# Two column tiles for the DeltaNet inverse's larger levels and for the samples' state products

## The chip, the cores and the metric

One Trainium2 chip, one NeuronCore of it. The metric is the device time of one execution in microseconds; of several runs the median is given.

## The reference

The reference is one layer of a streaming encoder for 256 prompt positions and 64 sample positions, 320 in all, with width 2048, in float32. It normalises, multiplies by one large input matrix, runs a convolution module beside a gated DeltaNet of 8 heads (head size 128), multiplies by an output matrix, and ends with a convolutional feed-forward block. The change lies in the DeltaNet, where for each chunk of positions a unit lower triangular matrix is inverted, and each sample head is started from a given state:

```python
m = jnp.where(strict, jnp.einsum('bhnid,bhnjd->bhnij', kb, k) * decay, 0.0)
tmat = lax.linalg.triangular_solve(m + eye, ..., left_side=True, lower=True, unit_diagonal=True)
...
def step(s, xs):
    v_new = u_c - jnp.einsum('bhld,bhde->bhle', w_c, s)
    o = jnp.einsum('bhld,bhde->bhle', qd_c, s) + jnp.einsum('bhij,bhje->bhie', qk_c, v_new)
    s = s * gl_c[..., None, None] + jnp.einsum('bhld,bhle->bhde', kd_c, v_new)
    return s, o
```

The kernel takes prompt chunks of 128 positions, and one sample chunk of 64 per head.

## The kernel before

The large products (input, output, up and down projection) run as dense streams on TensorE: a block of weights is 128x128 and stationary, the activations of all 320 positions stream past it. Each product is done three times on split numbers (high by high, low by high, high by low; lines 233, 234 and 237 of `block_matmul`). The weights come by DMA into `w`, ScalarE rounds them to `whi` (L217) and VectorE computes the rest `wlo` (L218); three buffers of each are kept.

The DeltaNet runs in between, in small steps. `tick` counts the dense matmuls, and after every 20 of them lets the jobs that are due issue their next step behind the last dense matmul; a `yield LAG_WAIT, ...` in a job says how many dense matmuls have to pass before its next step. So TensorE's order is fixed when the program is built: some dense matmuls, a group of small ones, dense ones again. The order on ScalarE and VectorE comes from the scheduler's own estimate and from priorities; each engine works its queue in order.

Heads go in pairs, four pairs in all. For one pair, `st` holds five instances (NI = 5): two prompt chunks of each of two heads (S_ = 4), and one instance in which the samples of the two heads stand one below the other, 64 rows each. `base_inverse` inverts the 16-row diagonal blocks on VectorE. `levels` then joins blocks to 32, 64 and 128 rows. In one level, for the two halves r0 (above) and r1 (below) of a block: `pz` = a product on the rows of r0, copied to `zq`; `px` and `py` = products of `zq` on the rows of r1, copied into `W` (the inverse, transposed) and `TT` (the inverse). `N` is the matrix `m`, tile `np`; `W` and `TT` are the two halves of tile `wtp`. The level that joins 16-row blocks is L792 to L808; the level of 32 rows is L815 (pz), L817 (copies to zq), L822 (px), L824 (py), L825 and L827 (copies); the level of 64 rows is L831, L832, L836, L837. All those products are float32.

Below, the partitions that a small matmul reads are called its row strip, those that it writes its column strip, and the two together its tile. In the code before, every instance of a level uses the same one or two tiles.

`post` uses the inverse. `vn0` is the first chunk's new values (`pvn`, L864). `ks` (L881) holds the samples' key and query products with the two states `s0`: both heads' samples (128 rows of `kqs`) are multiplied with both heads' states (256 columns), and of the result only the half is read in which a head's samples meet its own state. VectorE makes `rhs_` of it (L885) and ScalarE `qss` (L886), one instruction for each head. `rhs_` goes into `pvns` (L893).

Of the kernel before, what the change touches and what calls it, by code (L numbers as in the profile page):

```python
# [11 lines left out]
AF = mybir.ActivationFunctionType  # L12
ALU = mybir.AluOpType
# [4 lines left out]
P = 128  # L18
# [3 lines left out]
TS = 64  # L22
# [54 lines left out]
S_ = 4  # L77
# [23 lines left out]
def trunk_kernel(ctx, tc, ins, outs):  # L101
    nc = tc.nc
    V, S, G, PE = nc.vector, nc.scalar, nc.gpsimd, nc.tensor
# [94 lines left out]
    def cv(name, n=P, m=P):  # L198
        o, _ = CST[name]
        return cst[0:n, o:o + m] if o < NCST1 else cst2[0:n, o - NCST1:o - NCST1 + m]  # L200
# [115 lines left out]
    with tc.tile_pool(name="xp", bufs=1) as xp:  # L316
# [71 lines left out]
        for k0 in range(0, KB, 2):  # L388
            hi, lo = pre[k0 // 2]
            for ks in ((k0,), (k0 + 1,)) if k0 < 4 else ((k0, k0 + 1),):  # L390
                for wt in (hi, lo):
                    for k in ks:
                        for i, b in enumerate(FIRST):
                            ps = ready[b][:, 0:T]
                            o = (k - k0) * FW + i * P
# [214 lines left out]
    NI = S_ + 1  # L610
# [166 lines left out]
    zq = gd.tile([P, NI, TS], F32, tag="zq", bufs=1, name="zq")  # L777

    def levels(st):
        N, W, TT = st["np"], st["w"][:, 0, :, :], st["w"][:, 1, :, :]  # L780

        def out(name, n, w):
            return ps_g.tile([P, 512], F32, tag="g", name=name)[:, 0:n * w].rearrange("p (a w) -> p a w", a=n)


        q = [slice(32 * i, 32 * i + 32) for i in range(4)]
        even = [slice(32 * i, 32 * i + 16) for i in range(4)]
        odd = [slice(32 * i + 16, 32 * i + 32) for i in range(4)]
        pz = out("pz", NI, 16)
        for a in range(NI):  # L790
            for r, c in zip(q, even):
                PE.matmul(pz[r, a, :], N[r, a, r], TT[r, a, c], start=True, stop=True)  # L792
        S.activation(zh, pz, AF.Identity, scale=cv("odd", P, 1))
        yield LAG_WAIT, 2, 0
        px, py = out("px", NI, 16), out("py", NI, 16)
        for a in range(NI):
            for r, e, c in zip(q, even, odd):
                PE.matmul(px[e, a, :], zh[r, a, :], W[r, a, c], start=True, stop=True)
        for a in range(NI):
            for i, r in enumerate(q[:3]):  # L800
                if i != 1 or a < S_:
                    PE.matmul(py[r, a, :], W[r, a, r], zh[r, a, :], start=True, stop=True)
        for i, (r, e) in enumerate(zip(q, even)):
            if i < 3:
                n = S_ if i == 1 else NI
                V.tensor_tensor(TT[r, 0:n, e], TT[r, 0:n, e], py[r, 0:n, :], ALU.add)
        for i, (e, c) in enumerate(zip(even, odd)):
            S.copy(W[e, :, c], px[e, :, :])  # L808
        yield LAG_ADD, 1, 0

        pairs32 = (q[0:2], q[2:4])
        pz = out("pz", NI, 32)
        for a in range(NI):
            for r0, r1 in pairs32:
                PE.matmul(pz[r1, a, :], N[r0, a, r1], TT[r0, a, r0], start=True, stop=True)  # L815
        for r0, r1 in pairs32:
            S.copy(zq[r1, :, 0:32], pz[r1, :, :])  # L817
        yield LAG_WAIT, 2, 0
        px, py = out("px", NI, 32), out("py", S_, 32)
        for a in range(NI):  # L820
            for r0, r1 in pairs32:
                PE.matmul(px[r0, a, :], zq[r1, a, 0:32], W[r1, a, r1], start=True, stop=True)  # L822
        for a in range(S_):
            PE.matmul(py[q[1], a, :], W[q[1], a, q[1]], zq[q[1], a, 0:32], start=True, stop=True)  # L824
        S.copy(TT[q[1], 0:S_, q[0]], py[q[1], :, :])  # L825
        for r0, r1 in pairs32:
            S.copy(W[r0, :, r1], px[r0, :, :])  # L827
        yield LAG_ADD, 1, 0
        pz = out("pz", S_, 64)
        for a in range(S_):  # L830
            PE.matmul(pz[64:P, a, :], N[0:64, a, 64:P], TT[0:64, a, 0:64], start=True, stop=True)  # L831
        S.copy(zq[64:P, 0:S_, :], pz[64:P, :, :])  # L832
        yield LAG_WAIT, 1, 0
        px = out("px", S_, 64)
        for a in range(S_):
            PE.matmul(px[0:64, a, :], zq[64:P, a, :], W[64:P, a, 64:P], start=True, stop=True)  # L836
        S.copy(W[0:64, 0:S_, 64:P], px[0:64, :, :])  # L837

    def post(i, st):
        hh_ = (2 * i, 2 * i + 1)  # L840
        kq, kqs, kd, vh, at, W = st["kq"], st["kqs"], st["kd"], st["vh"], st["at"], st["w"][:, 0, :, :]
        kds = kdss[i % 2]
        rk, rq, irk, snb, cc, skd = (st["sc"][:, j, :] for j in range(6))
        eG, neG, eGl = gate["eG"], gate["neG"], gate["eGl"]

        def pair_tile(tag, n=2):
            return gd.tile([P, n, P], F32, tag=tag, bufs=1, name=tag)

        def bank(name, n):
            return ps_g.tile([P, 512], F32, tag="g", name=name)[:, 0:n * P].rearrange("p (a f) -> p a f", a=n)  # L850

        s0 = pair_tile("s0")
# [16 lines left out]
        def outputs(c, vn):  # L869
            p = bank("po", 4)  # L870
            for s in range(2):
                PE.matmul(p[:, 2 + s, :], kd[:, 2 * s + c, :], vn[:, s, :], start=True, stop=True)
            for s in range(2):
                PE.matmul(p[:, s, :], at[:, 2 * s + c, :], vn[:, s, :], start=True, stop=True)
            return p

        vn0 = new_values(0, [vh[:, 2 * s, :] for s in range(2)])

        p = bank("ks", 4)
        for j in range(2):  # L880
            PE.matmul(p[:, 2 * j:2 * j + 2, :], kqs[:, j, :], s0, start=True, stop=True)  # L881
        rhs_, qss = pair_tile("rhs", 1)[:, 0, :], pair_tile("qss", 1)[:, 0, :]
        for s in range(2):
            r = slice(s * TS, (s + 1) * TS)
            V.scalar_tensor_tensor(rhs_[r, :], p[r, s, :], neG[r, 2, hh_[1]:hh_[1] + 1], vh[r, S_, :], ALU.mult, ALU.add)  # L885
            S.activation(qss[r, :], p[r, 2 + s, :], AF.Identity, scale=eG[r, 2, hh_[1]:hh_[1] + 1])  # L886
        yield LAG_WAIT, 2, 0
        p = outputs(0, vn0)
        sn0 = pair_tile("sn0")
# [2 lines left out]
        p = bank("pvns", 1)  # L892
# [6 lines left out]
        p = bank("ks1", 4)  # L899
# [8 lines left out]
        p = bank("pos", 3)  # L908
# [11 lines left out]
        p = outputs(1, vn1)  # L920
# [21 lines left out]
        for s in range(2):  # L942

            pt = ps_t.tile([P, 512], F32, tag="t", name="pt_o")
            o = TP - s * TS
# [15 lines left out]
    def pair(i, st):  # L961
        while any(s not in st for s in range(NS)):
            yield GAP, 0, 0
        yield from base_inverse(i, st)
        yield LAG_BASE - 5 * GAP, 1, 0
        yield from levels(st)
        while i and any(j is pairs[i - 1] for j in jobs):
            yield GAP, 2, 0
        yield LAG_WAIT, 2, 0
        yield from post(i, st)  # L970
# [75 lines left out]
    for n in range(KB):  # L1046
# [11 lines left out]
        for j in range(nk2):  # L1058
            xh, xl = bx(K1 + j)
            o = j * P  # L1060
# [164 lines left out]
    for step in PLAN_Y.split():  # L1225
        how, ks = step[0], step[1:]
# [97 lines left out]
```

## Time and profile before

| | |
|---|---|
| median of three runs | 1489.62 us (1489.47 to 1491.08) |
| the profiled execution's own time | 1489.37 us |
| its span, first to last instruction | 1487.6 us |
| TensorE busy, share of the span | 1478.6 us, 99% |
| VectorE busy | 996.6 us, 67% |
| ScalarE busy | 730.8 us, 49% |
| the four visits to the levels and to `post` | between 160 and 427 us |
| in 160 to 420 us: VectorE busy, ScalarE busy | 225.7 and 146.6 of 260 us |

Busy times of TensorE overlap, since its matmuls are pipelined: a group of small matmuls is read by its starts, not by its busy time. In the profile's rows PE is TensorE, PEld its weight loads, DVE is VectorE, ACT is ScalarE, SP the engine that issues DMAs; L815 is line 815 of the kernel before. A row of the timeline merges consecutive instructions of one line; its second column reaches from the first start to the last end. A bracket at the end of a row gives the idle time ahead of the first of them and who ended it.

### The profile page before, as it was taken

The numbers are of one execution on the slowest core, as the hardware profiler recorded it, in microseconds if no ns is written. First come the engines' busy times: TensorE is split into PE (matmuls) and PEld (weight loads), VectorE is DVE, ScalarE is ACT, GpSimd is POOL, SyncE is SP. The second block draws the span as 40 slices with busy tenths as digits, with TensorE's granted clock in tenths as the row PEclk, the third lists the DMA queues.
The fourth block names the chain that finished last, engine by engine and source line by source line (L and its number), as shares of the span: only waits on it lengthen the run. The fifth ranks groups of instructions, "written<-read, shape, count | busy, mean of one in ns | idle before, by whom it ended". The sixth has DMA issues, their size and how long they took to land.

```text
span 1487.6 us, 27264 instructions
## 1 busy us (share of the span) xinstructions
PE 1478.6 (99%) x10610; PEld 1458.2 (98%) x10610; DVE 996.6 (67%) x1816; ACT 730.8 (49%) x1331; POOL 230.5 (15%) x390
## 2 busy tenths in 40 slices
PE   9999999999999999999999999999999999999998
PEld 8999999999999989999999999999999999999997
DVE  6779888888989678756336665545666545656554
ACT  7674556655454656544334444334444334444453
POOL 0111101021010000322002322002232001223101
PEclk9999999999999999999999999999999999999999
DMA  8435453544444734444554444554444455444453
GB/s 294 140 115 167 158 151 110 147 156 138 129 122 145 238 128 146 146 156 121 153 168 155 145 154 135 143 162 158 156 143 147 136 148 168 153 156 143 136 148 119
DMA packets 98281, 224.22 MB, mean 151 GB/s; under 512 B 18792, under 2 KB 39528, under 8 KB 98152
## 3 DMA queue, kind: packets, MB, share of 16 engines
q1 hardware_dynamic: 98008, 222.45, 47.8%
q8 instruction: 83, 1.36, 0.4%
q14 instruction: 46, 0.38, 0.1%
q10 hardware_dynamic: 144, 0.03, 0.0%
HBM read 215.33 MB, written 7.12 MB: 150 GB/s over the span
## 4 chain that ended last, share of the span: by engine, by line
PE 95%; ACT 2%; DVE 1%; issue 1%; DMA 0%; POOL 0%; DVEq 0%; ACTq 0%; POOLq 0%
PE psu L237 13%; PE psu L234 13%; PE psu L233 13%; PE psdn L233 7%; PE psdn L234 7%; PE psdn L237 7%; PE psq L233 3%; PE psq L234 3%; PE psq L237 3%; PE psm L237 2%; PE psm L233 2%; PE psm L234 2%; PE psu L1117 1%; PE psv L233 1%; PE psgate L233 1%; PE ps_first L398 1%
## 5 line engine op out<-in xcount | busy, mean ns | idle before, releaser
L217 ACT CAST whi<-w 128x1024 fp32r<-128x1024 f32 (+2 forms) x440 | 412.6, 940 | 488.5 <-PE psu L234 169.7
L218 DVE TENSOR_TENSOR wlo<-w,whi 128x1024 fp32r<-128x1024 f32 (+2 forms) x440 | 477.2, 1085 | 191.4 <-ACT whi L217 123.9
L233 PE MATMUL psu<-hi,whi 128*128 128x320 f32 x1344 | 397.0, 309 | 0.0
L234 PE MATMUL psu<-lo,whi 128*128 128x320 f32 x1344 | 396.9, 309 | 0.0
L234 PEld LDWEIGHTS psu<-lo,whi 128*128 128x128 f32 x1344 | 252.3, 188 | 0.0
L233 PEld LDWEIGHTS psu<-hi,whi 128*128 128x128 f32 x1344 | 252.2, 188 | 0.0
L237 PE MATMUL psu<-hi,wlo 128*128 128x320 f32 x1344 | 224.4, 309 | 0.0
L237 PEld LDWEIGHTS psu<-hi,wlo 128*128 128x128 f32 x1344 | 204.1, 188 | 0.0
L234 PE MATMUL psdn<-gl,whi 128*128 128x320 f32 x660 | 195.9, 310 | 0.0
L1150 POOL COPY nffn<-fbuf 128x2 f32<-128x2 f32 x88 | 99.5, 1131 | 586.7 <-DVE fbuf L1148 583.5
L1148 DVE TENSOR_TENSOR fbuf<-psu,rb 128x256 f32<-128x256 f32 x88 | 37.4, 424 | 169.1 <-PE psu L237 169.0
L233 PE MATMUL psdn<-gh,whi 128*128 128x320 f32 x480 | 142.8, 309 | 0.0
L234 PEld LDWEIGHTS psdn<-gl,whi 128*128 128x128 f32 x660 | 123.9, 188 | 0.3
L233 PE MATMUL psq<-hh,whi 128*128 128x320 f32 x352 | 106.0, 314 | 0.0
L234 PE MATMUL psq<-hl,whi 128*128 128x320 f32 x352 | 104.1, 309 | 0.0
L233 PEld LDWEIGHTS psdn<-gh,whi 128*128 128x128 f32 x480 | 90.1, 188 | 0.0
L237 PE MATMUL psdn<-gh,wlo 128*128 128x320 f32 x480 | 89.9, 309 | 0.0
L237 PEld LDWEIGHTS psdn<-gh,wlo 128*128 128x128 f32 x480 | 75.3, 188 | 0.0
L233 PEld LDWEIGHTS psq<-hh,whi 128*128 128x128 f32 x352 | 66.1, 188 | 0.4
L234 PEld LDWEIGHTS psq<-hl,whi 128*128 128x128 f32 x352 | 66.1, 188 | 0.2
L563 DVE SCALAR_TENSOR_TENSOR cvt<-ub,par,cvt 128x320 f32<-128x320 f32 x120 | 65.3, 545 | 0.1
L1193 DVE TENSOR_TENSOR y<-y,psdn 128x320 f32<-128x320 f32 x45 | 22.0, 488 | 58.7 <-PE psdn L237 58.7
(356 smaller groups left out, 2485.2 us busy)
## 6 DMA issues: line engine op xcount, KB each, us to landing
w<-in_w_up SPq DMA_DIRECT2D x176, 512.0 KB
w<-in_w_in SPq DMA_DIRECT2D x88, 512.0 KB
w<-in_w_down SPq DMA_DIRECT2D x64, 384.0 KB
w<-in_w_down SPq DMA_DIRECT2D x64, 320.0 KB
w<-in_w_out SPq DMA_DIRECT2D x32, 320.0 KB
w<-in_w_out SPq DMA_DIRECT2D x16, 384.0 KB
w<-in_w_first SPq DMA_DIRECT2D x6, 512.0 KB
wtp<-wsp SPq DMA_DIRECT2D x4, 640.0 KB
```

What stands on the lines that cost most here:

```text
L217: S.copy(hi[:, 0:width], w[:, 0:width])
L218: V.tensor_tensor(lo[:, 0:width], w[:, 0:width], hi[:, 0:width].bitcast(F32), ALU.subtract)
L233: tick(PE.matmul(ps, wh, xh, start=(first and k0 + j == 0), stop=False))
L234: tick(PE.matmul(ps, wh, xl, start=False, stop=False))
L237: tick(PE.matmul(ps, lo[:, j * P:(j + 1) * P], xh, start=False, stop=(final and k0 + j == nk - 1)))
L398: tick(PE.matmul(ps, w, xh, start=(k == 0 and wt is hi), stop=(k == KB - 1 and wt is lo)))
L563: return lambda: V.scalar_tensor_tensor(acc, x, w, acc, ALU.mult, ALU.add)
L1117: PE.matmul(pss[i][:, 0:T], wt[:, o:o + P], x, start=(k == 0 and n == 0), stop=(k == KB - 1 and n == 2))
L1148: V.tensor_tensor(buf[:, 2:258], psu[:, 0:TP], rb2[:, 0:TP], ALU.mult)
L1150: G.tensor_copy(nffn[:, b, 0, :], buf[:, 256:258])
L1193: V.tensor_tensor(y[:, n, :], y[:, n, :], psd[:, 0:T], ALU.add)
```

## The change

In the levels of 32 and 64 rows, instance `a` writes its product to one column strip if `a` is even and to another if it is odd. In the 32-row level `pz` goes to the strip of r1 or r0, `px` to that of r0 or r1, `py` to the third or fourth strip. In the 64-row level the two halves alternate. So half of the products land in PSUM on other partitions than those on which they are needed, and ScalarE's copies, one for the even and one for the odd instances, bring them there: a copy reads 32 or 64 partitions and writes others. Six copies per visit become twelve, each of half the instances or so.

The samples' state products are done for each head alone: 64 rows of `kqs` with that head's 128 state columns, written to the 64 partitions of that head's samples. So `ks` has two columns of 128 where it had four, and `rhs_` and `qss` are one instruction of 128 partitions each.

```diff
         for a in range(NI):
-            for r0, r1 in pairs32:
-                PE.matmul(pz[r1, a, :], N[r0, a, r1], TT[r0, a, r0], start=True, stop=True)
-        for r0, r1 in pairs32:
-            S.copy(zq[r1, :, 0:32], pz[r1, :, :])
+            for rs in pairs32:
+                PE.matmul(pz[rs[1 - a % 2], a, :], N[rs[0], a, rs[1]], TT[rs[0], a, rs[0]], start=True, stop=True)
+        for rs in pairs32:
+            for o in range(2):
+                S.copy(zq[rs[1], o:NI:2, 0:32], pz[rs[1 - o], o:NI:2, :])
         yield LAG_WAIT, 2, 0
         px, py = out("px", NI, 32), out("py", S_, 32)
         for a in range(NI):
-            for r0, r1 in pairs32:
-                PE.matmul(px[r0, a, :], zq[r1, a, 0:32], W[r1, a, r1], start=True, stop=True)
+            for rs in pairs32:
+                PE.matmul(px[rs[a % 2], a, :], zq[rs[1], a, 0:32], W[rs[1], a, rs[1]], start=True, stop=True)
         for a in range(S_):
-            PE.matmul(py[q[1], a, :], W[q[1], a, q[1]], zq[q[1], a, 0:32], start=True, stop=True)
-        S.copy(TT[q[1], 0:S_, q[0]], py[q[1], :, :])
-        for r0, r1 in pairs32:
-            S.copy(W[r0, :, r1], px[r0, :, :])
+            PE.matmul(py[q[2 + a % 2], a, :], W[q[1], a, q[1]], zq[q[1], a, 0:32], start=True, stop=True)
+        for o in range(2):
+            S.copy(TT[q[1], o:S_:2, q[0]], py[q[2 + o], o:S_:2, :])
+        for rs in pairs32:
+            for o in range(2):
+                S.copy(W[rs[0], o:NI:2, rs[1]], px[rs[o], o:NI:2, :])
         yield LAG_ADD, 1, 0
+        half = (slice(0, 64), slice(64, P))
         pz = out("pz", S_, 64)
         for a in range(S_):
-            PE.matmul(pz[64:P, a, :], N[0:64, a, 64:P], TT[0:64, a, 0:64], start=True, stop=True)
-        S.copy(zq[64:P, 0:S_, :], pz[64:P, :, :])
+            PE.matmul(pz[half[1 - a % 2], a, :], N[0:64, a, 64:P], TT[0:64, a, 0:64], start=True, stop=True)
+        for o in range(2):
+            S.copy(zq[64:P, o:S_:2, :], pz[half[1 - o], o:S_:2, :])
...
-            PE.matmul(px[0:64, a, :], zq[64:P, a, :], W[64:P, a, 64:P], start=True, stop=True)
-        S.copy(W[0:64, 0:S_, 64:P], px[0:64, :, :])
+            PE.matmul(px[half[a % 2], a, :], zq[64:P, a, :], W[64:P, a, 64:P], start=True, stop=True)
+        for o in range(2):
+            S.copy(W[0:64, o:S_:2, 64:P], px[half[o], o:S_:2, :])
...
-        p = bank("ks", 4)
+        p = bank("ks", 2)
         for j in range(2):
-            PE.matmul(p[:, 2 * j:2 * j + 2, :], kqs[:, j, :], s0, start=True, stop=True)
+            for s in range(2):
+                r = slice(s * TS, (s + 1) * TS)
+                PE.matmul(p[r, j, :], kqs[:, j, r], s0[:, s, :], start=True, stop=True)
...
-        for s in range(2):
-            r = slice(s * TS, (s + 1) * TS)
-            V.scalar_tensor_tensor(rhs_[r, :], p[r, s, :], neG[r, 2, hh_[1]:hh_[1] + 1], vh[r, S_, :], ALU.mult, ALU.add)
-            S.activation(qss[r, :], p[r, 2 + s, :], AF.Identity, scale=eG[r, 2, hh_[1]:hh_[1] + 1])
+        V.scalar_tensor_tensor(rhs_, p[:, 0, :], neG[:, 2, hh_[1]:hh_[1] + 1], vh[:, S_, :], ALU.mult, ALU.add)
+        S.activation(qss, p[:, 1, :], AF.Identity, scale=eG[:, 2, hh_[1]:hh_[1] + 1])
```

What stands in the engines' queues now. ScalarE at the fourth visit, from the copies of the first 32-row product on; `zT` is the gate of a head, `un` and `sg` belong to the convolution module, `CAST whi` are the weights. Before:

```order
L217 CAST whi<-w 128x1024 x2
L817 COPY zq<-pz 32x5x32 x2
L959 ACTIVATE zT_5113<-zT_5113 128x320
L217 CAST whi<-w 128x1024
L827 COPY wtp<-px 32x5x32
L825 COPY wtp<-py 32x4x32
L827 COPY wtp<-px 32x5x32
L591 ACTIVATE un<-pt_c,gnm,grs 128x128 x3
```

And now:

```order
L217 CAST whi<-w 128x1024 x2
L818 COPY zq<-pz 32x3x32
L818 COPY zq<-pz 32x2x32
L818 COPY zq<-pz 32x3x32
L965 ACTIVATE zT_5136<-zT_5136 128x320
L818 COPY zq<-pz 32x2x32
L217 CAST whi<-w 128x1024
L830 COPY wtp<-px 32x3x32
L827 COPY wtp<-py 32x2x32 x2
L830 COPY wtp<-px 32x2x32
L830 COPY wtp<-px 32x3x32
L830 COPY wtp<-px 32x2x32
```

The two copies to `zq` are four, and the fourth stands behind the activation `zT`. In the other three visits the four stand together.

VectorE at the third visit, around the samples' `rhs`; `cvt` and `odd` are the convolution's taps, `tmp` and `wi` the base inverse of the next pair. Before:

```order
L218 TENSOR_TENSOR wlo<-w,whi 128x1024
L563 SCALAR_TENSOR_TENSOR odd<-ub_587,par,odd 128x320
L563 SCALAR_TENSOR_TENSOR cvt<-ub_587,par,cvt 128x320
L885 SCALAR_TENSOR_TENSOR rhs<-ks,neG,vh 64x128
L563 SCALAR_TENSOR_TENSOR odd<-ub_587,par,odd 128x320
L885 SCALAR_TENSOR_TENSOR rhs<-ks,neG,vh 64x128
L754 TENSOR_TENSOR tmp<-wi,dn 40x50
```

And now:

```order
L218 TENSOR_TENSOR wlo<-w,whi 128x1024
L563 SCALAR_TENSOR_TENSOR odd<-ub_587,par,odd 128x320
L891 SCALAR_TENSOR_TENSOR rhs<-ks,neG,vh 128x128
L754 TENSOR_TENSOR tmp<-wi,dn 40x50
L563 SCALAR_TENSOR_TENSOR cvt<-ub_587,par,cvt 128x320
```

One instruction takes the place of two and stands one tap earlier; the taps behind it move by a place. On TensorE no group changes its place: the order is that of before, with four `ks` matmuls of 64x128 where two of 128x256 stood. GpSimd's queue and the DMA queue have the same instructions in the same order.

## The prediction

> **What bounds the kernel now.** I read the page first: which engine is busy, and on whose work the chain that ended last lies.
>
> ```profile
> span 1487.6 us, 27264 instructions
> PE 1478.6 (99%) x10610; PEld 1458.2 (98%) x10610; DVE 996.6 (67%) x1816; ACT 730.8 (49%) x1331; POOL 230.5 (15%) x390
> ...
> PE 95%; ACT 2%; DVE 1%; issue 1%; DMA 0%; POOL 0%; DVEq 0%; ACTq 0%; POOLq 0%
> ```
>
> TensorE carries 95% of the chain. So a nanosecond that the change takes out of TensorE's stream is worth a nanosecond, as long as nobody else is then late. I take the next rows from the timeline of TensorE at the first of four visits (one per pair of heads) to the inverse's levels. Columns: start, time from the first start to the last end, engine, line, tiles, shape, count.
>
> ```profile
> 172.06 0.50 PE L815 MATMUL pz<-wtp,np 32*32 32x32 f32 x20
> ...
> 175.62 0.41 PE L822 MATMUL px<-wtp,zq 32*32 32x32 f32 x14
> 175.84 0.21 PE L824 MATMUL py<-zq,wtp 32*32 32x32 f32 x1
> 175.86 0.22 PE L822 MATMUL px<-wtp,zq 32*32 32x32 f32 x3
> 175.90 0.19 PE L824 MATMUL py<-zq,wtp 32*32 32x32 f32 x1
> 175.90 0.22 PE L822 MATMUL px<-wtp,zq 32*32 32x32 f32 x2
> 175.93 0.19 PE L824 MATMUL py<-zq,wtp 32*32 32x32 f32 x1
> 175.93 0.19 PE L822 MATMUL px<-wtp,zq 32*32 32x32 f32 x1
> 175.96 0.32 PE L824 MATMUL py<-zq,wtp 32*32 32x32 f32 x5
> ```
>
> The program has 10 matmuls on L815, and the trace 20 records: each float32 matmul is two passes. The last five passes of L824 run alone on one tile, one every (0.32 - 0.19) / 4 = 0.032 us, since one pass shows 0.19. L815 uses two row strips, hence two tiles of ten passes each; its starts spread over 0.50 - 0.19 = 0.31 us, that is ten passes at 0.032. So a tile takes one pass per 0.032 us, and tiles run beside each other.
>
> The rows from 175.84 on carry the whole forecast. L824 reads partitions 32 to 63 and writes partitions 32 to 63. Half of L822's matmuls read the same partitions 32 to 63 and write 0 to 31. L824's first three passes (175.84, 175.90, 175.93) fall among the last six of L822, and L822 does not slow down. Two column tiles on the same rows therefore did run at once.
>
> How often this is paid, by the rows of two lines (count, then min/median/max ns, then first and last start):
>
> ```profile
> L836 PE MATMUL px<-wtp,zq x32: 218/218/267, 186.3 to 407.1; 64*64 64x64 f32 x32
> L881 PE MATMUL ks<-s,kqs x16: 379/379/382, 190.4 to 411.7; 128*128 128x256 f32 x16
> ```
>
> 32 and 16 records are four visits of 8 and 4, from 186 to 412 us. The 32-row lines come in the same four visits.
>
> **The change part by part, TensorE.** The 32-row product (L815): instances 0, 2, 4 stay on their column tile, 1 and 3 go to a free one. The longest tile has 3 x 2 = 6 passes in place of 10, so 4 x 0.032 = 0.126 us go per visit.
>
> The 32-row second products (L822, L824): before, the starts run from 175.62 to 175.96 + 0.32 - 0.19 = 176.09, 0.47 us. After, L822 takes 6 passes, and L824 has two tiles of 4. L824's passes began when 14 of L822's 20 had begun; with four tiles that comes after about four passes a tile, at 0.13 us. Four passes more end the group at 0.27 to 0.28 us: 0.19 us saved. This has row strip 32 to 63 feeding up to four column strips; the trace shows two. If only two go at once, L824's eight passes last 0.25 us and the saving is 0.09 us.
>
> The 64-row products (L831, L836), from the timeline at 186 us:
>
> ```profile
> 186.29 0.68 PE L836 MATMUL px<-wtp,zq 64*64 64x64 f32 x8
> 186.89 0.41 PE L233 MATMUL psq<-hh,whi 128*128 128x320 f32 x1
> 187.15 0.30 PE L234 MATMUL psq<-hl,whi 128*128 128x320 f32 x1
> ```
>
> Eight passes stand on one tile; their starts spread over 0.68 - 0.22 = 0.46 us, 0.058 a pass after the first. With two tiles four passes go, less a few ns between the tiles: 0.227 us for each of the two lines, 0.454 a visit.
>
> The samples' state products (L881), which come behind L864 (rows of the first visit):
>
> ```profile
> 189.93 0.60 PE L864 MATMUL pvn<-vh,wtp 128*128 128x128 f32 x4
> 190.37 1.03 PE L881 MATMUL ks<-s,kqs 128*128 128x256 f32 x4
> 191.05 0.50 PE L233 MATMUL psq<-hh,whi 128*128 128x320 f32 x1
> 191.38 0.31 PE L234 MATMUL psq<-hl,whi 128*128 128x320 f32 x1
> ```
>
> Here the matmuls leave full-array form, and that has a price. Going from full-array to narrow tiles is shown elsewhere:
>
> ```profile
> 242.27 0.49 PE L578 MATMUL pt_c<-cst,cvt 128*128 128x128 f32 x3
> 242.69 0.68 PE L836 MATMUL px<-wtp,zq 64*64 64x64 f32 x8
> ```
>
> Full-array passes of 128 columns follow each other every (190.37 - 189.93) / 4 = 0.11 us. L578's third therefore starts at 242.49, and L836 comes 0.20 us behind it in place of 0.11: 0.09 us for the switch. Coming back costs 0.14 us from L836's last start (186.75) to the dense matmul and 0.26 to the next, 0.40; a stream of 128 columns in place of 64 adds 0.053, so 0.45 after the new ks. Today L881's last start is 191.40 - 0.38 = 191.02, and the second dense matmul comes 0.36 us later. Passes: four of 0.216 (1.03 - 0.38 over three steps) become four on each of two tiles of 0.11, the step of L864; the first pass of a narrow group shows 0.05 more. Before, from L864's last start: 0.11 + 3 x 0.216 + 0.36 = 1.12 us. After: 0.20 + 0.05 + 3 x 0.11 + 0.01 + 0.45 = 1.04. So 0.08 us go. No row shows column tiles with all 128 rows. If they overlap and the first pass hides, 0.13 go; if they don't, eight passes in a row make it 0.35 us dearer. I take 0.08, since L822 beside L824 is the nearest row.
>
> Sum per visit: 0.126 + 0.191 + 0.454 + 0.083 = 0.854 us, times four is 3.42 us.
>
> The rule that speaks against this is in the Trainium skill, page "TensorE: Matmul & The Clock Gate", Part 3, "What overlaps and what doesn't": a weight load overlaps a running matmul only if its row group is another one. By it the new column tiles, which share their rows, would gain nothing; the rows at 175.84 to 175.93 disagree. It is the third case below.
>
> **ScalarE and VectorE.** The copies out of PSUM are split in two. Their durations:
>
> ```profile
> L817 ACT COPY zq<-pz x8: 283/285/287, 172.6 to 393.3; 32x160 f32<-32x160 f32 x8
> L825 ACT COPY wtp<-py x4: 257/257/259, 176.5 to 397.3; 32x128 f32<-32x128 f32 x4
> L837 ACT COPY wtp<-px x4: 367/367/367, 187.6 to 407.4; 64x256 f32<-64x256 f32 x4
> ```
>
> 32 elements less make 28 ns less. So 96 and 64 elements take about 229 and 201 ns: each pair of zq or px copies grows from 570 to 860, py's from 257 to 402, each 64-row copy from 367 to 2 x 255. That is 0.29 + 0.29 + 0.15 + 0.29 = 1.0 us per visit on ScalarE, against which one activation of qss falls away. Half of the new copies go to other partitions than they read. No row has that; it can't be cheaper than the same elements in place, and I bound it at 0.47, the 128x320 activation below. Either hides: zq is copied by 393.6 at the last visit and read at 396.3 (rows below), 2.7 us later, and even four copies at 0.47 fit.
>
> VectorE does one rhs of 128 rows in place of two of 64:
>
> ```profile
> L885 DVE SCALAR_TENSOR_TENSOR rhs<-ks,neG,vh 64x128 f32<-64x128 f32 x8 | 2.8, 349 | 2.1 <-PE ks L881 1.5 <-ACT qss L886 0.4
> ```
>
> That is 0.35 us less per visit, and a wait between the two engines goes. None of it is on the chain.
>
> Behind the four visits the chain leaves TensorE once for long, at the output projection:
>
> ```profile
> 499.72 0.16 PE psm L1063
> 499.92 0.73 ACT whi L217
> ...
> 506.61 6.44 DMA w<-in_w_out
> ```
>
> That transfer is issued behind casts which begin 0.04 us after a matmul (499.92). So it moves forward with TensorE, and the gain passes through it.
>
> What is late next? At the last visit the fourth zq copy is now queued behind zT on ScalarE (front part, first order listing), and zT waits for VectorE. The rows of before, ScalarE, then TensorE, then VectorE:
>
> ```profile
> 393.00 0.59 ACT L817 COPY zq<-pz 32x160 f32<-32x160 f32 x2 [0.54 <-PE pz L815]
> 395.51 0.47 ACT L959 ACTIVATE zT<-zT 128x320 f32<-128x320 f32 x1 [1.92 <-DVE zT L958]
> ```
> ```profile
> 396.30 0.38 PE L822 MATMUL px<-wtp,zq 32*32 32x32 f32 x12
> ```
> ```profile
> 342.11 0.49 DVE L536 TENSOR_TENSOR sg<-psgate,rb 128x320 f32<-128x320 f32 x1 [0.35 <-PE psgate L237]
> 369.69 1.23 DVE L218 TENSOR_TENSOR wlo<-w,whi 128x1024 fp32r<-128x1024 f32 x1 [2.64 <-ACT whi L217]
> 394.99 0.49 DVE L958 TENSOR_TENSOR zT<-psz,rb 128x320 f32<-128x320 f32 x1
> ```
>
> In the times of before, the fourth copy would end at 395.98 + 0.20 = 396.18, 0.12 us ahead of L822. TensorE will come there 3 x 0.854 + 0.126 = 2.69 us earlier. So the copy must move as far, and it hangs on VectorE, which from 370 to 408 us is nearly without a gap:
>
> ```profile
> 370.00:408.00 38.00, 37.60 (x75) 1.00 0.41 123
> ```
>
> VectorE itself waited for TensorE at 342.11. By then 1.71 us of two visits and 0.77 of the third are saved, 2.48; with the shorter rhs behind it, 2.5 to 2.9. The copy is then 0 to 0.1 us late. I take 0.1 off: 3.3 us.
>
> **The rivals.**
>
> A, the forecast: 3.3 us less. The profiled execution took 1489.37 us, 1.8 of it outside the span; 3.3 off is 1486.1. The median of before, 1489.62, is 0.25 above that execution, so 1486.3. Own range: L824 at 0.09 saved and ks at nothing leave 2.6 us (1487.0); ks at 0.13 and no stall give 3.6 (1486.0); the runs of before spread over 1.6 us, which I let widen it to 1485.2 to 1487.6.
>
> B, given back at the last visit: VectorE does not follow, and zT holds the fourth copy and with it L822. If VectorE has gained only its own 0.35 by then, L822 stands for 2.69 - 0.12 - 0.35 = 2.2 us and 1.2 us of the gain are left: 1488.4. For it: 37.60 busy of 38 us. Against: the waits at 342.11 and 369.69, where VectorE could start earlier. It decides from about 2.6 us of lead on. The Trainium skill has this as a general warning ("TensorEngine Tiling (Array Packing)", "PSUM Bottleneck"): tiling speeds up TensorE and not the copies out of PSUM, which may become the bound. Here the copies' own time fits; only their place in the queue is tight.
>
> C, column tiles on the same rows don't overlap: the inverse's products gain nothing, and ks costs 0.35 more a visit, 1.4 us in all: 1491.0, slower. The decision lies in one pass: above 0.032 us per pass where two column tiles share rows. Against it stand L824's three passes among L822's.
>
> D, each change of column tile on the same rows empties the array, at 0.09 us as on the switch above. A visit has 4 changes in L815, 4 in L822, 1 into L824, 3 in it, 3 + 3 in the 64-row products and 3 in ks: 21 x 0.09 = 1.9 us, with C's 0.35 that is 2.25, four times 9.0: 1498.6. Against it: L824's first pass starts 0.02 us before one of L822's.
>
> **How the numbers follow.** A 0.73, B 0.14, C 0.09, D 0.04. The time is A's, 1486.3. The range, 1485.2 to 1489.2, holds A and B, 0.87, with their spread; C and D are left out. What a measurement of this kernel can tell from no change is about 0.2%, 3.0 us; A's 3.3 passes that only just. I give three quarters of A, 0.56, to faster; the rest of A, B and nearly all of C, 0.39, to within; D and a hundredth of C, 0.05, to slower.
>
> **What would show it.** Right: L815's starts over 0.19 us in place of 0.31, L822 with L824 over 0.28 in place of 0.47, the 64-row products over 0.23 in place of 0.46, ks in eight records of which two start nearly together, and the dense matmuls between them at their old pace. B shows as an idle of TensorE before the last L822, named after ScalarE. C shows as unchanged spreads and a ks of some 0.8 us, D as gaps of 0.09 us inside the groups. The forecast is also wrong if the groups shrink as said and the chain gains less than 2.6 us; then a wait elsewhere took it, and the list of waits must name it.

## The result and the profile after

The changed kernel takes 1485.87 us in the median of 12 runs, the kernel before 1489.62 in 12 runs beside them: 3.75 us less, ratio 0.9976 with a 95% interval of 0.9969 to 0.9983. The forecast was 1486.3; the interval, 2.5 to 4.6 us less, does not tell its 3.3 us from the 3.75. The profiled execution has a span of 1483.9 us in place of 1487.6, 3.7 less. Of the experiments below, one execution of the state products moved in full-array form took 2409.81 us at a granted clock of 0.56; it stands in that kernel's median, which is 1487.38 without it, and not in its ratio.

The page of the changed kernel, its busy times and the chain that ended last:

```profile
span 1483.9 us, 27312 instructions
PE 1474.3 (99%) x10626; PEld 1452.9 (98%) x10626; DVE 994.5 (67%) x1812; ACT 734.1 (49%) x1355; POOL 234.0 (16%) x390
...
PE 94%; ACT 2%; DVE 1%; DMA 1%; issue 1%; POOL 0%; SPq 0%; ACTq 0%; DVEq 0%
```

TensorE still carries the chain, with 4.3 us less of busy time. ScalarE has 24 instructions and 3.3 us more, and the chain does not show it. (The section on the change counts six copies a visit that become twelve; they are seven that become fourteen, 28 more in four visits, and four activations of `qss` are gone.)

Where the time came from is read from the timeline of TensorE at the first visit. The lines have moved: L823 and L825 are the former L822 and L824, L841 the former L836, L870 and L889 the former L864 and L881.

```profile
172.27 0.38 PE L815 MATMUL pz<-wtp,np 32*32 32x32 f32 x20
...
175.71 0.28 PE L823 MATMUL px<-wtp,zq 32*32 32x32 f32 x10
175.80 0.21 PE L825 MATMUL py<-zq,wtp 32*32 32x32 f32 x1
...
175.81 0.23 PE L823 MATMUL px<-wtp,zq 32*32 32x32 f32 x6
...
175.89 0.22 PE L825 MATMUL py<-zq,wtp 32*32 32x32 f32 x3
...
185.89 0.45 PE L841 MATMUL px<-wtp,zq 64*64 64x64 f32 x8
...
189.30 0.60 PE L870 MATMUL pvn<-vh,wtp 128*128 128x128 f32 x4
189.84 0.66 PE L889 MATMUL ks<-s,kqs 128*64 128x128 f32 x8
```

The starts of a group spread over its second column less one pass. L815: 0.38 - 0.19 = 0.19 us in place of 0.31. L823 with L825: 175.89 + 0.22 - 0.19 - 175.71 = 0.21 in place of 0.47. L841: 0.45 - 0.22 = 0.23 in place of 0.46. L825 reads partitions 32 to 63 like half of L823, and its first pass starts when 10 of L823's 20 have started; so four column strips work on these rows at once, and nothing slows down.

By single starts, that is the start of each pass in the trace, which the rows merge, the two kernels compare like this. "Cost" is from the start of the dense matmul ahead of a group to that of the third behind it, less three dense steps of 0.147 us, so that entry and return are in it.

| group at a visit | spread before, after (us) | cost before, after (us) | saved |
|---|---|---|---|
| L815 | 0.312, 0.186 | 0.633, 0.500 | 0.133 |
| L822 + L824, now L823 + L825 | 0.465, 0.220 | 0.784, 0.539 | 0.245 |
| L831, now L835 (with L595 beside it) | 0.457, 0.230 | 1.083, 0.857 | 0.226 |
| L836, now L841 | 0.457, 0.230 | 0.795, 0.576 | 0.219 |
| L864 + L881, now L870 + L889 | 1.091, 0.920 | 1.310, 1.232 | 0.078 |

That is 0.90 us a visit, 3.6 in four. Two fixed marks frame the four visits: the group of L683 that starts at 153 us (the line runs earlier and later too), and the last of the four groups of transposes of `ot` (L947, after the change L953), some 290 us later. Before, and after:

```profile
153.17 0.38 PE L683 MATMUL tkq<-cst,kq 128*128 128x128 f32 x2
...
445.60 0.82 PE L947 MATMUL pt_o<-cst,ot 128*128 128x128 f32 x6
```
```profile
153.38 0.38 PE L683 MATMUL tkq<-cst,kq 128*128 128x128 f32 x2
...
442.22 0.82 PE L953 MATMUL pt_o<-cst,ot 128*128 128x128 f32 x6
```

445.60 - 153.17 = 292.43 us; 442.22 - 153.38 = 288.84: 3.59 less. Nearly the whole gain lies between the marks. Compared start for start, the 1620 dense matmuls between them come earlier by steps behind these five groups, and no other step is above 0.03 us but one, 0.05 the other way, behind L908 at the first visit. I call this stretch "the visits" below; it is far sharper than a run's time.

Copies to `zq` and the new `rhs`, by shape, in the changed kernel:

```profile
L818 ACT COPY zq<-pz x16: 202/218/233, 172.9 to 393.0; 32x96 f32<-32x96 f32 x8, 32x64 f32<-32x64 f32 x8
L891 DVE SCALAR_TENSOR_TENSOR rhs<-ks,neG,vh x4: 346/350/352, 193.7 to 408.9; 128x128 f32<-128x128 f32 x4
```

Here the copies of 64 elements cross partitions and those of 96 do not, and none takes over 5 ns longer than the size alone lets expect (229 and 201 ns were estimated for 96 and 64 elements). `rhs` on 128 partitions takes as long as it took on 64.

The place of rival B, the fourth copy behind `zT` at the last visit. VectorE, ScalarE and TensorE:

```profile
392.02 0.49 DVE L964 TENSOR_TENSOR zT<-psz,rb 128x320 f32<-128x320 f32 x1
```
```profile
392.55 0.47 ACT L965 ACTIVATE zT<-zT 128x320 f32<-128x320 f32 x1 [1.44 <-DVE zT L964]
393.03 0.21 ACT L818 COPY zq<-pz 32x64 f32<-32x64 f32 x1
```
```profile
393.69 0.28 PE L823 MATMUL px<-wtp,zq 32*32 32x32 f32 x10
```

The copy ends at 393.24, L823 starts at 393.69: 0.45 us to spare, and no wait. VectorE came 394.99 - 392.02 = 2.97 us earlier, TensorE 396.30 - 393.69 = 2.61. Both are counted from the start of the span; the changed kernel reaches the first mark 0.21 us later, so from there VectorE gained 3.18 and TensorE 2.82.

### The profile page after: what moved, and what is told of

Its sections match the earlier page's. It is cut to its first block, busy times and chain, and to the rows that moved or that the text cites. A ratio compares the mean times of both kernels' runs of the same rounds, so it can differ in the third digit from the quotient of the medians.

```text
span 1483.9 us, 27312 instructions
## 1 busy us (share of the span) xinstructions
PE 1474.3 (99%) x10626; PEld 1452.9 (98%) x10626; DVE 994.5 (67%) x1812; ACT 734.1 (49%) x1355; POOL 234.0 (16%) x390
## 4 chain that ended last, share of the span: by engine, by line
PE 94%; ACT 2%; DVE 1%; DMA 1%; issue 1%; POOL 0%; SPq 0%; ACTq 0%; DVEq 0%
PE psu L237 13%; PE psu L234 13%; PE psu L233 13%; PE psdn L233 7%; PE psdn L234 7%; PE psdn L237 7%; PE psq L233 3%; PE psq L234 3%; PE psq L237 3%; PE psm L233 2%; PE psm L234 2%; PE psm L237 2%; PE psu L1123 1%; PE psv L233 1%; PE psgate L233 1%; PE psgate L237 1%
```

## The experiments

Eight kernels were made; the changed kernel itself was run once more beside three of them. Each was timed against the kernel before. The visits, by the marks above:

| kernel | visits (us) | against before | median, before beside it (us) | ratio and interval |
|---|---|---|---|---|
| before | 292.43 | | | |
| changed | 288.84 | -3.59 | 1485.87, 1489.62 | 0.9976 [0.9969, 0.9983] |
| changed, again | 288.78 | -3.65 | 1485.64, 1489.46 | 0.9973 [0.9963, 0.9984] |
| 32-row level alone | 291.00 | -1.43 | 1488.46, 1489.21 | 0.9997 [0.9988, 1.0005] |
| 64-row level alone | 290.61 | -1.82 | 1487.59, 1489.21 | 0.9988 [0.9979, 0.9997] |
| state products alone | 292.11 | -0.32 | 1488.88, 1489.21 | 1.0000 [0.9992, 1.0009] |
| split copies, one strip | 292.59 | +0.16 | 1489.53, 1489.21 | 1.0006 [0.9997, 1.0015] |
| even instances first | 289.09 | -3.34 | 1485.97, 1489.46 | 0.9977 [0.9968, 0.9985] |
| state products moved | 288.35 | -4.08 | 1485.45, 1489.46 | 0.9971 [0.9960, 0.9981] |
| moved, full-array form | 291.19 | -1.24 | 1487.43, 1489.46 | 0.9988 [0.9980, 0.9997] |
| L825 on one strip | 289.28 | -3.15 | 1485.88, 1489.27 | 0.9975 [0.9966, 0.9985] |

### The three parts alone

The 32-row level alone (the rest as before):

```diff
-                PE.matmul(pz[r1, a, :], N[r0, a, r1], TT[r0, a, r0], start=True, stop=True)
+                PE.matmul(pz[rs[1 - a % 2], a, :], N[rs[0], a, rs[1]], TT[rs[0], a, rs[0]], start=True, stop=True)
...
-            PE.matmul(py[q[1], a, :], W[q[1], a, q[1]], zq[q[1], a, 0:32], start=True, stop=True)
+            PE.matmul(py[q[2 + a % 2], a, :], W[q[1], a, q[1]], zq[q[1], a, 0:32], start=True, stop=True)
```

> The kernel before with the change in the 32-row level alone; the 64-row level and the samples' state products as before. Array theory (a tile takes a pass per 0.032 us at 32 columns, tiles run beside each other, every pass taken off the longest tile comes off TensorE's stream): starts of the first 32-row product spread over 0.186 us, those of the second products over 0.220, the 64-row products over 0.457 each; per visit 0.133 + 0.245 = 0.378 us less, four times 1.5, so about 1488.1 us. Rival (the gain comes from the work that ScalarE and VectorE are spared at rhs and qss): no gain, 1489.6 or more, since ScalarE has four to six copies more here and nothing is spared.

Spreads 0.185 and 0.219, the 64-row products 0.457 as before; the visits are 1.43 us shorter, by the array theory 1.51. The median is 0.75 lower, and the ratio's interval holds no change. The last visit tells where the 0.08 went. VectorE, ScalarE and TensorE of this kernel:

```profile
393.67 0.49 DVE L961 TENSOR_TENSOR zT<-psz,rb 128x320 f32<-128x320 f32 x1
```
```profile
394.19 0.47 ACT L962 ACTIVATE zT<-zT 128x320 f32<-128x320 f32 x1 [1.94 <-DVE zT L961]
394.68 0.20 ACT L818 COPY zq<-pz 32x64 f32<-32x64 f32 x1
```
```profile
394.83 0.34 PE L823 MATMUL px<-wtp,zq 32*32 32x32 f32 x10
```

The fourth copy ends at 394.88, 0.05 us after L823 has begun; L823's first ten passes stretch from 0.28 to 0.34 us. Rival B is real here, at 0.06 us.

The 64-row level alone:

```diff
-            PE.matmul(pz[64:P, a, :], N[0:64, a, 64:P], TT[0:64, a, 0:64], start=True, stop=True)
+            PE.matmul(pz[half[1 - a % 2], a, :], N[0:64, a, 64:P], TT[0:64, a, 0:64], start=True, stop=True)
```

> The kernel before with the change in the 64-row level alone. Array theory: the two 64-row products' starts spread over 0.230 us each in place of 0.457, the 32-row groups over 0.312 and 0.465 as before; per visit 0.22 + 0.22 = 0.445 us less, four times 1.8, so about 1487.8 us. Rival (the gain is work spared at rhs and qss): no gain, 1489.6 or more.

Spread 0.45 - 0.22 = 0.23 us at the first visit, as in the changed kernel:

```profile
185.76 0.45 PE L838 MATMUL px<-wtp,zq 64*64 64x64 f32 x8
```

The visits are 1.82 us shorter and the median 1.6 lower, with an interval below 1. The array theory stands.

The samples' state products alone:

```diff
-            PE.matmul(p[:, 2 * j:2 * j + 2, :], kqs[:, j, :], s0, start=True, stop=True)
+            for s in range(2):
+                r = slice(s * TS, (s + 1) * TS)
+                PE.matmul(p[r, j, :], kqs[:, j, r], s0[:, s, :], start=True, stop=True)
```

> The kernel before with the change in the samples' state products alone. Array theory: the group with pvn and ks costs 1.23 us in place of 1.31, 0.08 a visit, 0.3 in all: 1489.3 us, which a median does not tell from no change; the levels' spreads stay at 0.312, 0.465, 0.457, 0.457. Rival (the gain is ScalarE's and VectorE's spared work and the wait between them): most of the 3.7 us, 1486 to 1487.

```profile
189.99 0.60 PE L864 MATMUL pvn<-vh,wtp 128*128 128x128 f32 x4
190.53 0.66 PE L883 MATMUL ks<-s,kqs 128*64 128x128 f32 x8
```

The rows have the shape of the changed kernel's, the visits are 0.32 us shorter, the time is not told from no change. The rival, by which ScalarE's and VectorE's spared work makes the gain, is out. The three parts add up: 1.43 + 1.82 + 0.32 = 3.57 against 3.59 and 3.65 for all together.

### The copies without the strips

```diff
-                PE.matmul(pz[rs[1 - a % 2], a, :], N[rs[0], a, rs[1]], TT[rs[0], a, rs[0]], start=True, stop=True)
+                PE.matmul(pz[rs[0], a, :], N[rs[0], a, rs[1]], TT[rs[0], a, rs[0]], start=True, stop=True)
...
-            PE.matmul(px[half[a % 2], a, :], zq[64:P, a, :], W[64:P, a, 64:P], start=True, stop=True)
+            PE.matmul(px[half[1], a, :], zq[64:P, a, :], W[64:P, a, 64:P], start=True, stop=True)
```

> The changed kernel's levels with their split copies, which cross partitions, and their instruction order, but all instances of a product on one and the same column strip (the other one), and the samples' state products as before. Array theory: the gain is gone, since the longest tile has as many passes as before: spreads 0.312, 0.465, 0.457, 0.457 and 1489.6 us within 0.5. Rival (what gains is the split of the copies, so that a part of the instances goes on earlier, or the changed order on ScalarE): 1486 to 1487. If the copies across partitions cost something on the chain, it shows here bare: over 1490.

TensorE at the first visit, and ScalarE and TensorE at the last:

```profile
172.24 0.50 PE L815 MATMUL pz<-wtp,np 32*32 32x32 f32 x20
...
186.47 0.68 PE L841 MATMUL px<-wtp,zq 64*64 64x64 f32 x8
```
```profile
395.82 0.47 ACT L965 ACTIVATE zT<-zT 128x320 f32<-128x320 f32 x1 [2.31 <-DVE zT L964]
396.30 0.34 ACT L818 COPY zq<-pz 32x96 f32<-32x96 f32 x2
```
```profile
396.46 0.57 PE L823 MATMUL px<-wtp,zq 32*32 32x32 f32 x15
```

All spreads are the old ones and the gain is gone. What splits and crosses partitions costs one thing on the chain: two copies now stand behind `zT`, the second ends at 396.64, and the group of L823 costs 0.961 us in place of 0.784. That 0.18 is the whole +0.16. So in the levels the gain is the passes that run beside each other; neither the split copies nor ScalarE's new order give any of it.

### The order of the instances

```diff
-        for a in range(NI):
+        for a in (0, 2, 4, 1, 3):
```

and `(0, 2, 1, 3)` for four instances, in all five products.

> The changed kernel with the instances issued even ones first, then odd ones, so that consecutive instances stand on one column tile. Same passes per tile. Theory of a short look-ahead (TensorE holds about 7 passes that wait for a busy tile, and then the tile beside it starves): first 32-row product 0.230 us in place of 0.186, second products 0.31 in place of 0.22, 64-row unchanged at 0.23; per visit 0.13 us, in all 0.5 us dearer, 1486.4. Rival (the order does not matter, only the longest tile does): all spreads and the time as in the changed kernel, 1485.9. Rival (only the two neighbouring passes of one instance go together, no look-ahead): spreads as in the kernel before, 1489.5.

```profile
172.40 0.41 PE L815 MATMUL pz<-wtp,np 32*32 32x32 f32 x20
```

L815 spreads over 0.219 us, the second products over 0.253, the 64-row products over 0.237. The visits are 0.31 us longer than in the changed kernel run beside it (289.09 against 288.78); 0.5 was expected. The order matters, by less than the look-ahead of seven passes gave, and the time (1485.97 against 1485.64) does not tell it. The look-ahead is how far TensorE goes on to later passes while earlier ones wait for their tile, and the single starts show it. In this kernel the first odd instance's pass starts when 6 of the 12 passes ahead of it have started: three waited on each of two tiles. In the kernel before L824's first started with 6 of L822's waiting, three a tile; in the changed kernel L825's with 10 waiting on four tiles. So it is no fixed count: 6 passes wait on two tiles and 10 on four. Two and a half to three for each busy tile fits these three groups; no run tests it further.

### L825 on one strip

```diff
-            PE.matmul(py[q[2 + a % 2], a, :], W[q[1], a, q[1]], zq[q[1], a, 0:32], start=True, stop=True)
+            PE.matmul(py[q[2], a, :], W[q[1], a, q[1]], zq[q[1], a, 0:32], start=True, stop=True)
```

> The changed kernel with L825's four products on one column strip in place of two; everything else as in the changed kernel. This goes at the one term that came out larger than forecast. Theory (L825's tiles start when TensorE's look-ahead reaches them, about 0.10 us after the first pass of L823, and from there the longest tile counts): eight passes on one tile end at 0.10 + 0.03 + 7 x 0.032 = 0.35, so the starts of L823 with L825 spread over 0.33 to 0.36 us in place of 0.220, 0.12 a visit, 0.5 us in all: 1486.4. Rival (as the forecast had it, L825 cannot begin before 14 of L823's passes have begun, and the rest of the saving is from elsewhere): it starts at 0.13 or later and the spread is 0.38 or more. Rival (row strip 32 to 63 feeds only so many column strips at once, so that one strip less costs nothing): 0.22 as before.

```profile
175.64 0.28 PE L823 MATMUL px<-wtp,zq 32*32 32x32 f32 x10
175.74 0.21 PE L825 MATMUL py<-zq,wtp 32*32 32x32 f32 x1
...
175.86 0.32 PE L825 MATMUL py<-zq,wtp 32*32 32x32 f32 x5
```

L825 starts 0.10 us after L823, as in the changed kernel, and its eight passes on one tile end the group: 0.339 us, inside 0.33 to 0.36. The visits are 0.50 longer than in the changed kernel's second profile (0.5 expected). Both rivals are out. The run's time, 1485.88, does not show 0.5 us.

### The state products moved behind the last 64-row product

Entry into narrow tiles and the return are paid twice, once for L841, once for L889. This kernel puts the state products directly behind L841, with `s0` loaded earlier:

```diff
+        p = out("ks", 2, P)
+        for j in range(2):
+            for s in range(2):
+                r = slice(s * TS, (s + 1) * TS)
+                PE.matmul(p[r, j, :], kqs[:, j, r], s0[:, s, :], start=True, stop=True)
         for o in range(2):
             S.copy(W[0:64, o:S_:2, 64:P], px[half[o], o:S_:2, :])
```

> The changed kernel with the samples' state products moved from behind pvn to right behind the last 64-row product of the levels (s0 is loaded earlier for it), so that one entry into narrow tiles and one return are paid in place of two. Theory (the state products' cost is mostly the entry and the return, some 0.35 us of the 0.79 that they cost behind pvn): 0.33 us less a visit, 1.3 us in all, 1484.5. Rival (what they cost is their passes): as the changed kernel, 1485.9. Rival (the new place brings a wait, for s0 or for the PSUM tile): over 1486.5, and the list of TensorE's waits names it.

```profile
185.84 0.45 PE L845 MATMUL px<-wtp,zq 64*64 64x64 f32 x8
186.22 0.66 PE L851 MATMUL ks<-s,kqs 128*64 128x128 f32 x8
```

The group costs 1.163 us, 0.587 more than L841 alone, while `pvn` alone falls from 1.232 to 0.447. So the move saves 0.2 us a visit, not 0.33: from the last start in 64x64 tiles to the first in tiles with 128 rows it is 0.148 us, and the step behind that is 0.05 longer than the next ones. From the full array the same two are 0.205 and 0.05. Of the 0.8 for four visits, 0.43 shows in the visits against the changed kernel's second profile. Some 0.22 of the rest went at the first visit, where the next products (L914) stand until 197.38, when ScalarE's copy `sn` is out, and their group costs 1.779 us in place of 1.561; the remaining 0.15 is not traced. ScalarE and TensorE:

```profile
196.98 0.35 ACT L902 COPY sn<-po 128x256 f32<-128x256 f32 x1
```
```profile
197.38 1.16 PE L914 MATMUL ks<-sn,kq 128*128 128x128 f32 x8
```

The median is the lowest of all, 1485.45, but 0.2 us below the changed kernel beside it is not told from no change.

The same move with the products in their old form (two matmuls of 128 rows by 256 columns, `rhs_` and `qss` per head):

```diff
-            for s in range(2):
-                r = slice(s * TS, (s + 1) * TS)
-                PE.matmul(p[r, j, :], kqs[:, j, r], s0[:, s, :], start=True, stop=True)
+            PE.matmul(p[:, 2 * j:2 * j + 2, :], kqs[:, j, :], s0, start=True, stop=True)
```

> The move of the run before with the samples' state products as in the kernel before: two matmuls of 128 rows by 256 columns, not on column tiles. If the entry and return are what the move saves, nothing is saved here, since these products stand in full-array form between the narrow ones and the dense ones: about 0.87 us a visit, as they cost in the kernel before, so 1486.2. If the move itself saves, whatever the form: 1484.5 to 1485.

The group costs 1.439 us, 0.863 more than L841 alone, as expected. The visits are 2.41 us longer than in the changed kernel's second profile: some 0.4 at these four groups, and the rest at three waits of TensorE, start for start 1.10, 0.55 and 0.33. Its list of waits names the first two:

```profile
PE po L891 <- ACT vn L885: 0.8, 1, 0.8
...
PE px L823 <- ACT zq L818: 0.3, 1, 0.3
```

The first: ScalarE's second `qss` waits for VectorE's second `rhs` and holds `vn` behind it. The second is rival B, at its largest here. ScalarE and TensorE:

```profile
394.67 0.20 ACT L818 COPY zq<-pz 32x64 f32<-32x64 f32 x1
```
```profile
394.32 0.26 PE L823 MATMUL px<-wtp,zq 32*32 32x32 f32 x6
394.92 0.23 PE L823 MATMUL px<-wtp,zq 32*32 32x32 f32 x4 [0.34 <-ACT zq L818]
```

L823 has begun, stands until the copy is out at 394.87, and the group costs 1.088 us in place of 0.539. The third is at the last visit: a dense matmul waits for `bl`, which VectorE makes late. VectorE, and TensorE's weight load:

```profile
410.28 0.48 DVE L242 TENSOR_TENSOR bl<-af,bh 128x320 fp32r<-128x320 f32 x1
```
```profile
410.81 0.19 PEld L234 LDWEIGHTS psm<-bl,whi 128*128 128x128 f32 x1 [0.34 <-DVE bl L242]
```

## Why the prediction was right, point by point

**The bound.** TensorE's stream was the bound, and what left it left the time: 3.59 us off the visits, 3.7 off the span, 3.75 off the median.

**L815**: 0.126 forecast, 0.133 measured. **The 64-row products**: 0.454 forecast, 0.445 measured. **The state products**: 0.083 forecast, 0.078 measured, from a sum of an entry, a return and passes for which no row had the tile form. Two column tiles that both read all 128 rows do overlap: the eight passes of L889 start within 0.66 - 0.28 = 0.38 us, where eight in a row at 0.11 would take 0.77.

**L822 with L824 is the term that was mis-sized**: 0.191 forecast, 0.245 measured. The step that was off is "with four tiles that comes after about four passes a tile, at 0.13 us". It carried over the count of 14 passes from the kernel before. What carries over better is the number of passes waiting for each tile, three before: with four tiles 10 of L823's passes wait when L825 begins, so it begins at 0.10 us. From there its own four passes a tile end the group, and the kernel with L825 on one strip shows that it is L825's tile that ends it. The bound of two column strips at once, 0.09, is out.

**The sum**: 0.854 a visit forecast, 0.90 measured; times four 3.42 and 3.6. This miss and the 0.1 us below went the same way, so the 3.3 fell short of the 3.59 of the visits; the rest up to 3.75 is within the spread of the medians.

**The 0.1 us for a late fourth copy did not come.** I had VectorE 2.5 to 2.9 us earlier; it came 2.97 earlier, and TensorE 2.61 in place of 2.69 (3.18 and 2.82 from the first mark). The lag from `zT`'s start on VectorE to that of L822 or L823 tells why:

| kernel | zT on VectorE | L822 or L823 | lag |
|---|---|---|---|
| before | 394.99 | 396.30 | 1.31 |
| 64-row level alone | 393.32 | 394.62 | 1.30 |
| 32-row level alone | 393.67 | 394.83 | 1.16 |
| state products alone | 394.31 | 396.12 | 1.81 |
| changed | 392.02 | 393.69 | 1.67 |

With the 64-row level alone TensorE is 1.7 us earlier and the lag is the old one: VectorE does follow TensorE. With the state products alone VectorE gains 0.5 on TensorE: that comes with the shorter `rhs`, the only change to its queue there. The changed kernel has both. B needed a VectorE that does not follow, and that is refuted. But its edge is there: the 32-row level without the shorter `rhs` waits 0.06 us, and kernels in which two copies stand behind `zT` or VectorE is late wait 0.18 and 0.55. The state products, worth 0.3 us themselves, also pay for this.

**C and D** are out: the spreads halved, and changes of column tile on the same rows cost 6 to 7 ns from start to start. The Trainium skill's rule ("TensorE: Matmul & The Clock Gate", Part 3, "What overlaps and what doesn't"), that a weight load overlaps a running matmul only with another row group, is contradicted here: L825's weights are loaded and used on row strip 32 to 63 while L823 runs on the same rows. The weight loads of the changed kernel at the first visit, beside the matmuls of L823 that start from 175.71 to 175.90:

```profile
175.70 0.20 PEld L823 LDWEIGHTS px<-wtp,zq 32*32 32x32 f32 x14 [0.19 <-issue]
175.80 0.10 PEld L825 LDWEIGHTS py<-zq,wtp 32*32 32x32 f32 x1
```

**What passes through.** Behind the marks, from the transposes of `ot` to L259, the kernel before takes 527.80 - 445.60 = 82.20 us, the changed one 81.89. In the other nine profiles this stretch has 80.8 to 85.0, with no relation to the visits that shows; it holds the waits for the transfers of `in_w_out`. Why it varies was not tried. Outside the visits and this stretch the eleven profiles differ by 0.9 us. So it is most of the spread between the profiled executions, and the reason why the parts alone are told by the visits and not by the medians.

## What to carry to other kernels

Count passes per tile, not matmuls: where a group of small products ends with one tile working alone, every second instance on a free column strip takes up to half of its passes away, and a copy that has to leave PSUM anyway brings the result to the right partitions in the time of a copy in place. Alternate the tiles in program order; the other order gave back 0.31 us of the visits here. Then look at where the added copies stand in their engine's queue, above all behind an instruction that waits for a third engine: their own time was harmless, that place cost TensorE from 0.06 to 0.55 us in three kernels.

## What the runs showed of the hardware

- Four column strips on one row strip run at once (L823 with L825), and TensorE goes on past passes that wait for a busy tile: past 6 on two tiles, past 10 on four.
- Moving data across partitions in a ScalarE copy costs nothing that shows: the copies of 32x96 to `zq` take 232 ns in place (changed kernel) and 229 across (split copies, one strip).
- From 64x64 tiles to tiles of 128 rows by 64 columns TensorE takes 0.148 us to the first start, where it takes 0.205 from the full array: a group that changes the form of its tiles pays again.
- TensorE's clock fell to about half for a while amid the stream in two of the eleven profiles (the kernel with the state products moved, and L825 on one strip). In the first, around waits of 1.00 and 1.21 us:

```profile
507.86 0.42 PE L1073 MATMUL psm<-bh,whi 128*128 128x320 f32 x1 [1.00 <-ACT whi L217]
...
509.63 0.42 PE L1075 MATMUL psm<-bh,wlo 128*128 128x320 f32 x1 [1.21 <-DVE wlo L218]
...
511.09 0.47 PE L1073 MATMUL psm<-bp,whi 128*128 128x320 f32 x1
```

The columns of the windows are length, TensorE's busy time, granted clock, DMA share and GB/s:

```profile
510.00:512.00 2.00, 2.00 (x11) 0.59 0.82 223
512.00:514.00 2.00, 2.00 (x10) 0.56 0.92 270
514.00:516.00 2.00, 2.00 (x16) 1.00 0.81 302
```

Twelve dense matmuls came 0.27 us behind each other in place of 0.147, 1.5 us in all. The second had waits of 1.14 and 1.07 us there. Other profiles had waits as long at this place and kept their clock (the kernel with one strip for all: 1.7 and 1.1 us), so what sets it off stays open.
